# A fourth group of seven products in each FFN, with the quadrants in activation buffers

## The chip, the cores and the metric

The kernel runs on one core of one Trainium2 chip. The metric is the device time of one execution in microseconds (us). Each kernel is timed in several runs, and the median is compared. One further execution is taken by the hardware profiler, and all profile lines come from it.

Engines are called as in the profile: PE is the matrix engine, PEld its weight loads, DVE the vector engine, ACT the scalar engine, POOL GpSimd, SP the engine whose queue issues most transfers.

## The reference

A hybrid encoder of two layers works on 256 tokens of width 1024 in float32. Each layer has a gated linear attention branch, a grouped-query attention branch, a merge with an output projection, a SwiGLU FFN of hidden width 2816, and a gated per-layer embedding. The part that the change touches is the FFN:

```
gate, up = jnp.split(rms_norm(h, g_ffn_pre) @ w_ffn_in, 2, axis=-1)
h = h + rms_norm((jax.nn.silu(gate) * up) @ w_ffn_out, g_ffn_post)
```

`w_ffn_in` is 1024 x 5632, `w_ffn_out` is 2816 x 1024. The attention output projection `w_o_attn` (1024 x 1024) uses the same machinery as the FFN groups.

## The kernel before

**Numbers in two parts.** Every float32 operand of a product is kept as a high part (rounded by a cast) and a low part (what the rounding left). One product is three matmuls: high by high, high by low, low by high (`mm3`). The 256 tokens are two halves of 128 (`hf`).

**Weight units.** All weights are streamed once, as units of 1 MB (512 x 512 elements, in a tile of 128 x 2048). A unit is loaded by SP's queue into one of two `raw` tiles, then cut into two halves of 1024 columns. For each half ACT casts the high part into `wh` (L113) and DVE subtracts to get the low part `wl` (L109). There are four pairs of `wh` and `wl` (pool `wp`), and `Stream` counts how many are in use (`held`): a unit is made as soon as fewer than `depth` (4) are held, and given back when PE is done with it (`done`). A plain unit costs PE 24 matmuls of 512 columns, 12 for each token half.

**Groups of seven.** Where two by two quadrants of weights meet two by two quadrants of activations, eight products of quadrants can be replaced by seven products of sums (`seven`, and on the side of the weights `Stream.step`). A product of the seven is 12 matmuls. The activations' sums are made once per FFN (`sums`). On the side of the weights a group has four quadrants x, z, y, q of 1 MB. Step 1 splits x, then adds z to it (DVE) and adds y to z (a DMA that accumulates, from SBUF to SBUF). Step 2 splits x and adds y to it (DVE). Step 3 splits x and then adds q to it by two accumulating DMAs of 512 KB straight from HBM. Steps 4 to 7 split y, z, q (loaded as a raw unit) and x. Accumulating DMAs are issued by POOL. So x must be split in step 3, have q added, and be split again in step 7. On the side of the results DVE and ACT combine the products (`first_half`, copies and subtractions at L629 to L638), after product 6 for the first token half and after product 7 for the second.

Before the change x and z lie in a lent pair of `wh` and `wl`, so three pairs are left for splitting while a group is worked on; y lies in a tile of the pool `big` (nine tiles of 1 MB, which hold activations). The loads of a group wait for `ws.lend`, which the last step of the group before sets.

**The FFN.** The 2816 hidden columns are 11 blocks of 256. Blocks 0 and 1 are worked first, as plain units, first for one token half and then for the other. The strings `FFN` give the order after that: `u` is half a plain block of `w_ffn_in` (24 matmuls), a digit is a step of a group (two blocks, 12 matmuls), `o` is a unit of `w_ffn_out` (24 matmuls), `p` prepares the embedding. Each string has one group. Before: groups for blocks 2/3, 6/7 and 8/9 (`PAIRS`), plain blocks 4, 5 and 10 (`PLAIN`). The last three units of `w_ffn_out` come after the strings, again one token half after the other. `OUT` is the order of the units of `w_ffn_out`. The gated hidden activations are transposed by DMA on SP's queue (`turn_words`), those of the last group by PE, and lie in `big` tiles (`hid`).

**What sets the order.** The program is written in the order in which PE works; steps of transposes and the like are put in after so many "ticks". A planner then places each engine's instructions by priority and readiness in its own estimate of time, and gives out buffers. Each engine, and each DMA queue, runs its list in order, waiting on semaphores.

Of the kernel before, what the change touches and what calls it, by code (L numbers as in the profile page):

```python
# [34 lines left out]

FFN = "uu1u2u34u567" "uo12o34o5o67" "poo12o345o67"
MERGE = "GGGG1G2G34G5G67gggg"
PLAIN, PAIRS = (4, 5, 10), (2, 6, 8)  # L40
OUT = (0, 1, 2, 3, 4, 5, 10, 6, 7, 8, 9)

WAIT_LAST = (3, 4)
SENT, LANDED, NEXT = 3, 9, 2
# [7 lines left out]
def trunk_kernel(ctx: ExitStack, tc: tile.TileContext, a: dict, out: bass.AP):  # L52
# [58 lines left out]
    def split(hi, lo, src):  # L111

        cast = nc.scalar.copy(hi, src)  # L113
        vsub(lo, src, hi.bitcast(F32))
        return cast
# [56 lines left out]
            )  # L172
        ]

    plan = []
    for l in range(DEPTH):
        w = a["w_in"][l]
        plan += [unit_rows(w, n, C_RA, C_RA + 1056, 2 if l + n == 0 else 1) for n in range(4)]
        for c0 in (C_AK, C_GQ, C_GK, C_GV, C_GV + 512, C_GG, C_GG + 512):
            plan += [unit(w, kh, c0) for kh in range(2)]  # L180
        gates = [unit(w, kh, c0) for c0 in (C_GA, C_GA + 512, C_GB, C_GB + 512) for kh in range(2)]
        glas = [unit(a["w_o_gla"][l], kh, j * 512) for j in range(2) for kh in range(2)]
        pair = [unit(a["w_o_attn"][l], kh, j * 512) for kh in range(2) for j in range(2)]
        for x in MERGE:
            plan.append(gates.pop(0) if x == "G" else glas.pop(0) if x == "g" else (pair, int(x)))
        plan += [unit(a["w_out"][l], kh, j * 512) for kh in range(2) for j in range(2)]
        w = a["w_ffn_in"][l]
        blocks = [[unit_gate_up(w, kh, b) for kh in range(2)] for b in range(NBLK)]
        plan += blocks[0] + blocks[1]
        plains = [u for b in PLAIN for u in blocks[b]]  # L190
        pairs = [[unit(w, kh, c + b * 256) for kh in range(2) for c in (0, HIDDEN)] for b in PAIRS]
        outs = [unit_rows(a["w_ffn_out"][l], n) for n in OUT]
        for x in FFN.replace("p", ""):
            if x == "1":
                pair = pairs.pop(0)
            plan.append(plains.pop(0) if x == "u" else outs.pop(0) if x == "o" else (pair, int(x)))
        plan += outs
        plan += [unit_rows(a["w_ple_proj"][l], 0)]
        plan += [unit(a["w_ple_gate"][l], kh, j * 512) for kh in range(2) for j in range(2)]
# [14 lines left out]
    class Stream:  # L214
# [8 lines left out]
        def __init__(self, depth):  # L223
            self.depth, self.held, self.room, self.ready, self.open = depth, 0, 0, [], False
            self.loads, self.jobs, self.lend = [], [], False
            pairs = {}
            for item in plan:
                if callable(item):
                    x = Load(item)
                    self.loads.append(x)  # L230
                    self.jobs.append(lambda x=x: self.plain(x))
                else:
                    units, n = item
                    if n == 1:
                        b11, b12, b21, b22 = units
                        x, z = (Load(b, lambda tag=tag: self.lent(tag), tag == "wh") for b, tag in ((b11, "wh"), (b12, "wl")))
                        y, q = Load(b22, big), Load(b21)
                        pairs[id(units)] = x, y, z, q
                        self.loads += [x, y, z]
                    if n == 5:  # L240
                        self.loads.append(q)
                    self.jobs.append(lambda p=pairs[id(units)], n=n: self.step(n, *p))

        def lent(self, tag):

            if tag == "wh":
                self.held += 1
                self.lend = False
            return wp.tile([P, UNIT], F32R, tag=tag, name=nm("lent")).bitcast(F32)

        def load(self, between=lambda: None):
# [30 lines left out]
        def plain(self, x):  # L282
            return self.put(x)

        def made(self, x):
            for piece in self.put(x):
                self.cast = split(*piece)

        def step(self, n, x, y, z, q):
            def add(to, other):  # L290
                c = slice(0, 2048)
                nc.vector.tensor_tensor(out=to.raw[:, c], in0=to.raw[:, c], in1=other.raw[:, c], op=ALU.add)

            def sent(to, src):
                nc.gpsimd.dma_start(to.raw[:, :2048], src, accum_op=ALU.add)

            if n == 7:
                self.load()
            self.made((x, x, x, y, z, q, x)[n - 1])
            if n == 1:  # L300
                add(x, z)
                sent(z, y.raw[:, :2048])
            elif n == 2:
                add(x, y)
            elif n == 3:
                for dst, src in q.make(x.raw):
                    for c in (slice(0, 2), slice(2, 4)):
                        nc.gpsimd.dma_start(dst[:, c], src[:, c], accum_op=ALU.add)
            elif n == 7:
                self.held -= 1  # L310
                self.lend = True

# [1189 lines left out]
```

## Time and profile before

| | |
|---|---|
| median of the runs | 920.76 us (920.49 to 921.4) |
| the profiled execution's own time | 921.25 us |
| span in its profile | 919.1 us |
| PE busy | 904.6 us, 98% |
| DVE busy | 737.2 us, 80% |
| ACT busy | 643.9 us, 70% |
| DMA moved | 193.38 MB, 210 GB/s |

The time of the profiled execution is 2.15 us more than its span, which lies around the first and last instruction. Matmuls overlap in PE, so the mean duration of one (about 390 ns) is longer than the pace at which they follow each other. The pace is read from the chain of waits, which gives a stretch of matmuls with its length and count. DVE's and ACT's instructions overlap a little too: the distance between starts is some 0.07 us shorter than the duration.

### The profile page before, as it was taken

The page shows a single profiled execution, that of the slowest core. Times are in us where ns is not written, and L with a number is a line of the kernel's source. Part 1 is how long each engine was busy: PE and PEld are TensorE (multiplying, and loading weights), DVE is VectorE, ACT ScalarE, POOL GpSimd, SP SyncE. Part 2 cuts the span into 40 slices and gives each one's busy share as a digit, 9 for nine tenths or more (in the row PEclk, how much of TensorE's full clock was granted, in tenths as well). Part 3 has the DMA queues.
Part 4 walks back from the last instruction along what each step waited for, and adds up shares of the span by engine and source line. Part 5 has one row for each costly group of instructions (what it writes and reads, how often), then busy time and mean ns, then how long its engine had stood idle before and what let it go on. Part 6 is the DMA issues. An engine that isn't in the chain of part 4 may idle for free.

```text
span 919.1 us, 12313 instructions
## 1 busy us (share of the span) xinstructions
PE 904.6 (98%) x4561; PEld 768.3 (84%) x4561; DVE 737.2 (80%) x947; ACT 643.9 (70%) x1032; POOL 112.4 (12%) x174
## 2 busy tenths in 40 slices
PE   8999999999999999999999999999999999999996
PEld 6999888888888888888899988888888788878786
DVE  4798987977679796888689789688786798968874
ACT  4658777964568796776665686878656787957663
POOL 2410201140010100010023002111001010101000
PEclk9999999999999999999999999999999999999999
DMA  6555356986489998966555524399675999979541
GB/s 218 182 193 180 117 163 231 229 241 234 144 243 256 279 273 250 301 194 240 184 176 184 190 91 148 128 290 234 208 247 173 274 230 290 261 284 243 200 167 46
DMA packets 123290, 193.38 MB, mean 210 GB/s; under 512 B 33431, under 2 KB 56471, under 8 KB 122206
## 3 DMA queue, kind: packets, MB, share of 16 engines
q1 hardware_dynamic: 117726, 175.81, 59.3%
q0 software_dynamic: 5504, 16.78, 10.1%
q8 instruction: 36, 0.59, 0.3%
q14 instruction: 24, 0.20, 0.1%
HBM read 175.80 MB, written 1.05 MB: 192 GB/s over the span
## 4 chain that ended last, share of the span: by engine, by line
PE 80%; ACT 6%; DMA 5%; DVE 4%; issue 2%; POOL 2%; SPq 0%; POOLq 0%; ACTq 0%; DVEq 0%
PE acc_0ffnin L97 10%; PE acc_1ffnin L97 10%; PE acc_0ffnin L581 5%; PE acc_1gate L97 5%; PE acc_0gate L97 5%; PE acc_1ffnin L581 4%; PE acc_1gqk L97 3%; PE acc_0rq L97 2%; PE acc_0gqk L97 2%; PE acc_1ple L97 2%; PE acc_1gg L97 2%; PE acc_0gg L97 2%; PE acc_0v L97 2%; PE acc_1v L97 2%; PE acc_1merge L97 2%; PE acc_0merge L97 2%
## 5 line engine op out<-in xcount | busy, mean ns | idle before, releaser
L97 PE MATMUL acc_1ffnin<-wh_1ffnin,big_1ffnin 128*128 128x512 f32 x176 | 56.5, 392 | 0.1
L97 PE MATMUL acc_0ffnin<-wh_0ffnin,big_0ffnin 128*128 128x512 f32 x176 | 56.2, 391 | 0.0
L109 DVE TENSOR_TENSOR wl_1ffnin<-raw_1ffnin,wh_1ffnin 128x1024 fp32r<-128x1024 f32 x38 | 44.9, 1220 | 12.3 <-ACT wh_1ffnin L113 12.3
L109 DVE TENSOR_TENSOR wl_0ffnin<-raw_0ffnin,wh_0ffnin 128x1024 fp32r<-128x1024 f32 x38 | 44.9, 1221 | 10.5 <-ACT wh_0ffnin L113 10.2
L113 ACT CAST wh_1ffnin<-raw_1ffnin 128x1024 fp32r<-128x1024 f32 x38 | 38.3, 1050 | 17.7 <-DMA raw_1ffnin<-in_w_ffn_out_dram 9.1
L113 ACT CAST wh_0ffnin<-raw_0ffnin 128x1024 fp32r<-128x1024 f32 x38 | 38.4, 1050 | 16.8 <-DMA raw_0ffnin<-in_w_ffn_out_dram 7.8
L109 DVE TENSOR_TENSOR wl_1ffnin<-lent_1ffnin,wh_1ffnin 128x1024 fp32r<-128x1024 f32 x30 | 35.5, 1220 | 4.9 <-ACT wh_1ffnin L113 4.7
L109 DVE TENSOR_TENSOR wl_0ffnin<-lent_0ffnin,wh_0ffnin 128x1024 fp32r<-128x1024 f32 x30 | 35.5, 1221 | 4.8 <-ACT wh_0ffnin L113 4.7
L97 PEld LDWEIGHTS acc_1ffnin<-wh_1ffnin,big_1ffnin 128*128 128x128 f32 x176 | 33.0, 188 | 7.2 <-ACT wh_1ffnin L113 0.5
L97 PEld LDWEIGHTS acc_0ffnin<-wh_0ffnin,big_0ffnin 128*128 128x128 f32 x176 | 33.0, 188 | 6.9 <-DVE big_0ffnin L109 0.2
L113 ACT CAST wh_1ffnin<-lent_1ffnin 128x1024 fp32r<-128x1024 f32 x30 | 30.3, 1049 | 8.6 <-issue 2.9
L113 ACT CAST wh_0ffnin<-lent_0ffnin 128x1024 fp32r<-128x1024 f32 x30 | 30.3, 1050 | 8.4 <-issue 2.9
L97 PE MATMUL acc_1ffnin<-wl_1ffnin,big_1ffnin 128*128 128x512 f32 x88 | 34.4, 391 | 0.8 <-DVE wl_1ffnin L109 0.8
L97 PE MATMUL acc_0ffnin<-wl_0ffnin,big_0ffnin 128*128 128x512 f32 x88 | 34.5, 392 | 0.3 <-DVE wl_0ffnin L109 0.3
L581 PE MATMUL acc_0ffnin<-wh_0ffnin,mid_0ffnin 128*128 128x512 f32 x96 | 31.0, 390 | 0.0
L581 PE MATMUL acc_1ffnin<-wh_1ffnin,mid_1ffnin 128*128 128x512 f32 x96 | 31.0, 390 | 0.0
L97 PE MATMUL acc_0ffnin<-wh_0ffnin,big_0wout 128*128 128x512 f32 x96 | 30.4, 389 | 0.0
L97 PE MATMUL acc_1ffnin<-wh_1ffnin,big_1wout 128*128 128x512 f32 x96 | 30.3, 389 | 0.0
L97 PE MATMUL acc_0rq<-wh_start,big_start 128*128 128x384 f32 (+1 forms) x96 | 25.4, 350 | 1.5 <-ACT big_start L124 1.5
L97 PE MATMUL acc_1rq<-wh_0ple,big_0ple 128*128 128x384 f32 (+1 forms) x96 | 23.5, 325 | 0.0
L581 PE MATMUL acc_1ffnin<-wh_1ffnin,big_1wout 128*128 128x512 f32 x72 | 23.1, 389 | 0.0
L581 PE MATMUL acc_0ffnin<-wh_0ffnin,big_0wout 128*128 128x512 f32 x72 | 23.1, 389 | 0.0
(745 smaller groups left out, 3011.7 us busy)
## 6 DMA issues: line engine op xcount, KB each, us to landing
raw_0ffnin<-in_w_ffn_out_dram SPq DMA_DIRECT2D x11, 1024.0 KB, 5.1
raw_1ffnin<-in_w_ffn_out_dram SPq DMA_DIRECT2D x11, 1024.0 KB, 5.1
lent_0ffnin<-in_w_ffn_in_dram SPq DMA_DIRECT2D x6, 1024.0 KB, 7.5
lent_1ffnin<-in_w_ffn_in_dram SPq DMA_DIRECT2D x6, 1024.0 KB, 6.0
raw_0rq<-in_w_in_dram SPq DMA_DIRECT2D x4, 1024.0 KB, 5.1
raw_0v<-in_w_in_dram SPq DMA_DIRECT2D x4, 1024.0 KB, 5.1
raw_0merge<-in_w_out_dram SPq DMA_DIRECT2D x4, 1024.0 KB, 5.2
raw_0wout<-in_w_ffn_in_dram SPq DMA_DIRECT2D x8, 512.0 KB, 4.6
```

The source lines that it names most:

```text
L97: return nc.tensor.matmul(o, lhsT, rhs, start=start, stop=stop)
L109: nc.vector.tensor_tensor(out=out, in0=in0, in1=in1, op=ALU.subtract)
L113: cast = nc.scalar.copy(hi, src)
L581: nc.tensor.matmul(o, x, y, start=first and k + n == 0, stop=k == 3 and n == 2, skip_group_check=not first)
```

## The change

- The strings `FFN` become four, each with one group: blocks 2/3, 4/5, 6/7 and 8/9. Only block 10 (and blocks 0 and 1) stay plain. Both half-blocks `u` and one `o` lie in the first string, two `o` in the second and third, three in the fourth. The units of `w_ffn_out` outside the strings are the same three. `OUT` is reordered so that block 10 comes third.
- x and z of the FFN groups (`roomy`) lie in `big` tiles, not in `wh`/`wl`; so all four pairs are there for splitting. `lend` is set after step 6. The group of `w_o_attn` keeps its lent pair.
- The sums of steps 1 and 2 are made by halves of 1024 columns, each right behind the split of that half.
- The third sum is made by DMA for every group in the list `added`; since that list holds them all, the other path (`n == 5 and not far`, a DVE sum) is not used.

```diff
-FFN = "uu1u2u34u567" "uo12o34o5o67" "poo12o345o67"
+FFN = "u1u2o34567" "1o2o34567" "p1o2o34567" "1o2o34o567"
-PLAIN, PAIRS = (4, 5, 10), (2, 6, 8)
-OUT = (0, 1, 2, 3, 4, 5, 10, 6, 7, 8, 9)
+PLAIN, PAIRS = (10,), (2, 4, 6, 8)
+ADDED = (2, 4, 6, 8)
+OUT = (0, 1, 10, 2, 3, 4, 5, 6, 7, 8, 9)
...
-        def lent(self, tag):
-
-            if tag == "wh":
-                self.held += 1
-                self.lend = False
+        def lent(self, tag, i):
+
+            self.lend = False
+            if i in roomy:
+                return big()
+            self.held += tag == "wh"
             return wp.tile([P, UNIT], F32R, tag=tag, name=nm("lent")).bitcast(F32)
...
-        def made(self, x):
-            for piece in self.put(x):
+        def made(self, x, other=None):
+            for j, piece in enumerate(self.put(x)):
                 self.cast = split(*piece)
+                if other:
+                    self.add(x, other, slice(j * 1024, (j + 1) * 1024))
...
-            self.made((x, x, x, y, z, q, x)[n - 1])
+            self.made((x, x, x, y, z, q, x)[n - 1], {1: z, 2: y}.get(n))
             if n == 1:
-                add(x, z)
                 sent(z, y.raw[:, :2048])
-            elif n == 2:
-                add(x, y)
-            elif n == 3:
+            elif n == 3 and far:
                 for dst, src in q.make(x.raw):
                     for c in (slice(0, 2), slice(2, 4)):
                         nc.gpsimd.dma_start(dst[:, c], src[:, c], accum_op=ALU.add)
-            elif n == 7:
+            elif n == 5 and not far:
+                self.add(x, q)
+            elif n == 6 and roomy_:
+                self.lend = True
+            elif n == 7 and not roomy_:
                 self.held -= 1
                 self.lend = True
```

More of the change, by code (lines that the diff above doesn't have):

```diff
@@ L173, in unit_rows @@
         ]
-    plan = []
+    plan, added, roomy = [], [], []
     for l in range(DEPTH):
@@ L183, in trunk_kernel @@
         pair = [unit(a["w_o_attn"][l], kh, j * 512) for kh in range(2) for j in range(2)]
+        added.append(id(pair))
         for x in MERGE:
@@ L195, in trunk_kernel @@
                 pair = pairs.pop(0)
+                roomy.append(id(pair))
+                if PAIRS[-1 - len(pairs)] in ADDED:
+                    added.append(id(pair))
             plan.append(plains.pop(0) if x == "u" else outs.pop(0) if x == "o" else (pair, int(x)))
@@ L235, in __init__ @@
                         b11, b12, b21, b22 = units
-                        x, z = (Load(b, lambda tag=tag: self.lent(tag), tag == "wh") for b, tag in ((b11, "wh"), (b12, "wl")))
+                        x, z = (Load(b, lambda tag=tag, i=id(units): self.lent(tag, i), tag == "wh") for b, tag in ((b11, "wh"), (b12, "wl")))
                         y, q = Load(b22, big), Load(b21)
@@ L241, in __init__ @@
                         self.loads.append(q)
-                    self.jobs.append(lambda p=pairs[id(units)], n=n: self.step(n, *p))
-        def lent(self, tag):
-            if tag == "wh":
-                self.held += 1
-                self.lend = False
+                    self.jobs.append(lambda p=pairs[id(units)], n=n, f=id(units) in added, r=id(units) in roomy: self.step(n, f, r, *p))
+        def lent(self, tag, i):
[3 more added lines that the diff above has]
+            self.held += tag == "wh"
             return wp.tile([P, UNIT], F32R, tag=tag, name=nm("lent")).bitcast(F32)
@@ L283, in plain, with add, step @@
             return self.put(x)
-        def made(self, x):
-            for piece in self.put(x):
+        def made(self, x, other=None):
+            for j, piece in enumerate(self.put(x)):
                 self.cast = split(*piece)
[L289 to L292, printed above, removed]
+                if other:
+                    self.add(x, other, slice(j * 1024, (j + 1) * 1024))
+        def add(self, to, other, c=slice(0, 2048)):
+            nc.vector.tensor_tensor(out=to.raw[:, c], in0=to.raw[:, c], in1=other.raw[:, c], op=ALU.add)
+        def step(self, n, far, roomy_, x, y, z, q):
             def sent(to, src):
```

## The prediction, made before the change was run

> **What bounds the kernel now.** I read the page first, then PE's waits, the chain of waits, the busy time by stretches of the FFN, and the order of time on DVE and POOL.
>
> ```profile
> span 919.1 us, 12313 instructions
> PE 904.6 (98%) x4561; PEld 768.3 (84%) x4561; DVE 737.2 (80%) x947; ACT 643.9 (70%) x1032; POOL 112.4 (12%) x174
> ...
> PE acc_1ffnin L97 <- DVE wl_1ffnin L109: 0.8, 1, 0.8
> ...
> PE acc_0ffnin L97 <- DVE wl_0ffnin L109: 0.3, 1, 0.3
> ```
>
> PE is the bound, and in the FFN it waits for the weights' low parts hardly at all. The chain gives PE's pace:
>
> ```profile
> 266.28 24.94 PE acc_0ffnin L97 x107
> 291.22 2.72 PE acc_0ffnin L581 x12
> ```
>
> Twelve matmuls, one product of a group, take 2.72 us; a plain unit of 24 takes 5.44. The first group begins at 291.22 behind two plain units, so the first string begins at 280.3. The strings of layer 0 by stretches (length; busy PE, PEld, DVE, ACT, POOL; clock; DMA share; GB/s), and the last two of layer 1:
>
> ```profile
> 280.18:326.42 46.24, 46.24 (x205) 38.30 (x204) 40.43 (x44) 37.34 (x52) 3.42 (x3) 1.00 0.97 253
> 326.42:373.38 46.96, 46.69 (x206) 38.38 (x205) 38.14 (x38) 34.64 (x42) 3.29 (x3) 1.00 0.92 282
> 373.38:414.68 41.30, 41.30 (x186) 34.19 (x185) 36.84 (x34) 30.74 (x35) 4.31 (x4) 1.00 0.85 232
> ...
> 775.30:823.10 47.80, 46.98 (x206) 38.37 (x205) 38.65 (x38) 35.52 (x43) 3.36 (x3) 1.00 0.94 278
> 823.10:866.50 43.40, 42.70 (x192) 35.04 (x191) 37.48 (x36) 31.40 (x37) 3.33 (x3) 1.00 0.86 243
> ```
>
> PE is full, but DVE is busy 81 to 89% and the DMA engines 85 to 97%. Whatever shortens PE's work here and lengthens theirs meets them soon.
>
> **What the change removes.** Blocks 4 and 5 were four plain units, 21.76 us of PE; as a group they are seven products, 19.04. That saves 2.72 us in each layer, 5.44 in all. It is worth this only if PE stays fed.
>
> **What it adds on DVE and ACT.** Three more splits per layer, two weight sums, the group's result sums. The rows:
>
> ```profile
> 276.35 2.37 DVE L109 TENSOR_TENSOR wl_0ffnin<-raw_0wout,wh_0ffnin 128x1024 fp32r<-128x1024 f32 x2 [0.51 <-ACT wh_0ffnin L113]
> ...
> 298.08 2.35 DVE L109 TENSOR_TENSOR wl_0ffnin<-raw_0ffnin,wh_0ffnin 128x1024 fp32r<-128x1024 f32 x2
> 300.36 0.42 DVE L109 TENSOR_TENSOR big_0ffnin<-mid_0ffnin,big_0ffnin 128x256 fp32r<-128x256 f32 x1
> 300.69 2.35 DVE L109 TENSOR_TENSOR wl_0ffnin<-lent_0ffnin,wh_0ffnin 128x1024 fp32r<-128x1024 f32 x2
> ...
> 331.19 0.69 DVE L106 TENSOR_TENSOR t_0ffnin<-mid_0ffnin,t_0ffnin 128x512 f32<-128x512 f32 x1
> 331.79 2.29 DVE L292 TENSOR_TENSOR lent_0ffnin<-lent_0ffnin,lent_0ffnin 128x2048 f32<-128x2048 f32 x1
> 333.99 0.75 DVE L106 TENSOR_TENSOR t_0ffnin<-acc_0ffnin,t_0ffnin 128x256 f32<-128x256 f32 x2
> ...
> 342.71 2.36 DVE L109 TENSOR_TENSOR wl_0ffnin<-lent_0ffnin,wh_0ffnin 128x1024 fp32r<-128x1024 f32 x2
> ```
>
> By starts, a unit's two subtractions take 2.28 us, 1.14 a half; a 512-column operation 0.60, a 256-column one 0.33, a whole weight sum 2.20. A sum by halves isn't in the trace; a subtraction of 1024 columns has the same shape, so 1.14, and two halves cost 0.08 more than the whole: nothing. What halves may gain is that the next cast needn't await the whole sum; I count that as nothing too, at most one cast (1.05, below) in each of steps 1 and 2 where DVE waits.
>
> New second string, "1o2o34567": PE 7 x 2.72 + 2 x 5.44 = 29.92 us. DVE: nine units 20.52, four half sums 4.56, three result sums, two gate products and two splits of turned activations, seven times 0.60 = 4.2; together 29.3. The old second string confirms it: 38.14 busy, less three units (6.84) and a plain block's products and split (about 1.3), is 30.0 by durations. So DVE has no slack in the two inner strings. ACT: 34.64 less three units of two casts (6.3) is 28.3 or less, some slack. In the first string PE has 35.36, in the last 35.36 with a DVE need of 31.6.
>
> **Buffers and loads.** Nine `big` tiles: u2 two, up to three `hid` tiles alive, x, y, z of this group, and x of the next before this one ends. Tiles of consumed hidden blocks come free as each `o` ends, in time for the next z and y; I cost this at nothing, covered by the 13.6 us or more of products 3 to 7 between that `o` and the next group. The loads wait in SP's queue only for these tiles; the raw loads and transposes stand behind them there, so a late tile costs those a wait as well.
>
> **The loop that decides.** x is split in step 3, has q added by DMA, and is split again in step 7, now with only steps 4, 5, 6 in between. Before, a plain unit or two lay there as well.
>
> ```profile
> 344.30 2.41 POOL L308 DMA_DIRECT2D lent_0ffnin<-in_w_ffn_in_dram  x2 [8.71 <-DVE wl_0ffnin L109]
> ...
> lent_0ffnin<-in_w_ffn_in_dram POOLq DMA_DIRECT2D x2, 512.0 KB, 10.3
> ...
> lent_0ffnin<-in_w_ffn_in_dram POOLq DMA_DIRECT2D x2, 512.0 KB, 11.1
> ...
> lent_0ffnin<-in_w_ffn_in_dram POOLq DMA_DIRECT2D x2, 512.0 KB, 7.5
> ...
> lent_1ffnin<-in_w_ffn_in_dram POOLq DMA_DIRECT2D x2, 512.0 KB, 10.0
> ...
> lent_1ffnin<-in_w_ffn_in_dram POOLq DMA_DIRECT2D x2, 512.0 KB, 12.3
> ...
> lent_1ffnin<-in_w_ffn_in_dram POOLq DMA_DIRECT2D x2, 512.0 KB, 8.2
> ...
> DMA to landing us min/median/max: 6.1/9.1/13.6
> ...
> L113 ACT CAST wh_0ffnin<-raw_0ffnin 128x1024 fp32r<-128x1024 f32 x38 | 38.4, 1050 | 16.8 <-DMA raw_0ffnin<-in_w_ffn_out_dram 7.8
> ```
>
> The lines with KB are the landing times of the six groups in order, three for each layer; the line below them is over all sixteen such DMAs, the attention projection's too. The first half's DMA is issued at 344.30, 0.45 after the first subtraction begun at 342.71 gives way (342.71 + 1.14 = 343.85); the second 1.2 later, that is 0.5 after the unit's split. With landing time A, step 7's second half is cast (1.05) and subtracted (1.14) by 0.5 + A + 2.2 after step 3. DVE's list then runs on in order: one result sum 0.6, step 1 4.56 and two 512s 1.2, `o` 2.28, step 2 4.56 and one 0.6, `o` 2.28, two turned splits 1.2, step 3 2.28: 19.56. The loop takes A + 22.3 us, and PE's string 29.92. Up to A = 7.6 it costs nothing; above, each turn falls back by A - 7.6.
>
> There are three turns per layer (from each string's step 3 to the next one's). DVE enters with a lead: from 276.35 it has to do u, 1, u, 2, o, 3 (18.2), five operations of 512 for the activations' sums (3.0), four turned splits and three products of 256 (2.3), so is done at 299.9; PE comes to step 3 at 280.3 + 21.8 = 302.1, and needs only the first half, 1.14 earlier. Lead 3.3.
>
> The DMA wait isn't seen in this position, so its bounds: 7.5 (the emptiest neighbour) gives no stall; 12.3 (behind two or three fresh loads) gives 3 x 4.7 - 3.3 = 10.8 us per layer. I take 9.1, the median of all sixteen, one below the FFN groups' own: before, each step 3 had a raw load and a y just issued ahead of it; now the next group's loads go out earlier, as their tiles come free. Stall 3 x 1.5 - 3.3 = 1.2 per layer, 2.4 in all.
>
> [...]
>
> **Sum.** 921.25 (the profiled execution: 919.1 and 2.15 around it) - 5.44 + 2.4 = 918.2; the median of the runs stands 0.49 below that execution, so **917.7 us**, 3.1 (0.33%) faster.
>
> **Rivals.** *Fully hidden.* If A stays under 8.7, three turns eat no more than the lead: 920.76 - 5.44 = 915.3. For it: 7.5 in the third group. Against: DVE's waits of ACT, which I left out.
>
> *The accumulating DMA takes the place of the plain units (slower).* Place: cast of step 7 waiting for x, with DVE and ACT behind it in order. It outweighs the gain when three turns cost 2.72 + 3.3 = 6.0 per layer, that is 2.0 each, A above 9.6. At A = 10.3: 4.8 per layer, 920.76 - 5.44 + 9.6 = 924.9; at 11.1: 7.2 and 929.7. For it: four of the six groups landed at 10.0 or later. Against: the lead may be larger with four split pairs instead of three.
>
> *The DMA engines themselves become the bound.*
>
> ```profile
> q0 software_dynamic: 688, 2.10, 24.4%
> ```
>
> One group's accumulations took 24.4% of the second string, 11.5 us of all sixteen engines. Shares of the three old strings: 0.97 x 46.24 + 0.92 x 46.96 + 0.85 x 41.30 = 123.2 us. With 11.5 more it is 134.7, against PE's new 130.6. If none of it moves ahead of the strings, 4.1 per layer is lost: 920.76 - 5.44 + 8.2 = 923.5; if x and z of the first group go ahead of it (two loads of 1.05 MB, 6.8 us at the second string's 282 GB/s over its share 0.92), nothing is lost. Half of it, 919.4, is no change that can be told.
>
> *The change does not do what it says*: nine tiles don't suffice and x arrives late. Then the old pattern returns, one wait of a raw load (7.8 us of ACT's idle in 38 casts, little of it reaching PE): about 921.
>
> **Chances.** Forecast 0.40; hidden 0.17; slower by the loop 0.27; DMA bound or tiles late 0.16. Within 0.2% (1.84 us, about what a measurement of this kernel can tell from no change) fall part of the forecast's own spread (a landing 0.4 longer adds 2.4 us) and most of the last case. Faster 0.46, same 0.22, slower 0.32. The likeliest case alone holds 916 to 921; the range for 8 in 10 reaches from just under the hidden case to the crowded landing: 914.8 to 927.
>
> **What would show it.** PE: 24 fewer matmuls in all, 4537. DVE in the inner strings over 95% busy. A wait of ACT's cast in step 7 for an accumulating DMA, and behind it PE waits on `wl` in steps 1 and `o` of the next string: small if right, 4 us or more per layer if the slower rival is. Landing of the accumulating DMAs near 9. If DVE's idle time is before other casts than step 7's, the loop is the wrong cause. If PE waits for raw or `big` loads, it is the DMA engines or the tiles.

## The result, and the profile after

The changed kernel takes 953.79 us (median of 4 runs, 949.25 to 957.09); the kernel before, beside it, 920.85 us (920.49 to 921.4). The ratio is 1.0361, with a 95% interval of 1.0338 to 1.0383: it is 3.6% slower, where 917.7 us was forecast.

The head of the page of the changed kernel:

```profile
span 951.9 us, 12344 instructions
PE 911.1 (96%) x4537; PEld 769.0 (81%) x4537; DVE 761.1 (80%) x985; ACT 656.2 (69%) x1042; POOL 116.7 (12%) x180
```

PE has its 24 matmuls less (4537 instead of 4561) and is busy 6.5 us longer. At the pace of before 4537 matmuls would be 904.6 x 4537 / 4561 = 899.8 us, so the matmuls have become slower, by 11.3 us in all (not evenly: in the turns below, those at a clock of 1.00 have 0.228 to 0.229 us of busy time for each, close to the 0.226 and 0.227 of the first two strings of layer 0 before; those at 0.91 to 0.95 have 0.234 to 0.244). PE's idle time rose from 919.1 - 904.6 = 14.5 us to 40.8. Against the span that the change was to give (919.1 - 5.44 = 913.7) 38.2 us are missing.

They are missing in the strings of the FFN. The third sum of a group is issued once per string, so the distance from one such issue to the next is one turn of the loop that the prediction described. The changed kernel by these turns, three in layer 0 and three in layer 1 (columns as in the prediction's table of strings):

```profile
296.14:330.12 33.98, 31.65 (x138) 25.56 (x137) 30.34 (x33) 27.51 (x35) 3.34 (x3) 1.00 0.83 213
330.12:366.07 35.95, 32.40 (x135) 26.00 (x134) 29.60 (x30) 25.61 (x30) 3.31 (x4) 0.95 1.03 267
366.07:400.53 34.46, 31.86 (x140) 25.39 (x139) 30.05 (x31) 26.03 (x31) 3.32 (x3) 1.00 0.93 254
756.20:791.76 35.56, 31.54 (x138) 25.36 (x138) 30.43 (x33) 28.45 (x38) 3.33 (x3) 1.00 0.85 215
791.76:829.36 37.60, 32.43 (x133) 26.27 (x131) 29.55 (x30) 25.63 (x30) 3.35 (x4) 0.91 1.03 253
829.36:865.01 35.65, 33.03 (x141) 27.01 (x140) 30.05 (x31) 25.93 (x31) 3.31 (x4) 0.95 0.92 249
```

The six turns last 213.2 us; PE needs 6 x 29.92 = 179.5. That is 33.7 us, nearly all of the loss. PE, DVE and ACT all have idle time in every turn: none of them is the bound. The DMA engines' share is 0.83 to 1.03 (the reckoning can come out over 1); what that is worth is taken up below.

The chain of waits of the changed kernel (start, length, what was under way), its entries of a DMA in the FFN:

```profile
297.26 11.56 DMA big_0ffnin<-in_w_ffn_in_dram
331.32 14.01 DMA big_0ffnin<-in_w_ffn_in_dram
367.19 12.60 DMA big_0ffnin<-in_w_ffn_in_dram
400.19 7.31 DMA mid_0ffnin<-t_0ffnin
...
752.12 11.35 DMA mid_1ffnin<-t_1ffnin
792.90 15.72 DMA big_1ffnin<-in_w_ffn_in_dram
830.48 13.78 DMA big_1ffnin<-in_w_ffn_in_dram
864.66 14.94 DMA mid_1ffnin<-t_1ffnin
```

The five `big` entries are the second of the two accumulating DMAs of a group, issued 1.1 to 1.2 us behind the first; the three `mid` entries are DMA transposes of turned activations. The longest waits of ACT and of PE (us in all, times, longest), in the profile's views of waits:

```profile
ACT mid_1ffnin L435 <- DMA mid_1ffnin<-t_1ffnin: 25.9, 5, 10.1
ACT mid_0ffnin L435 <- DMA mid_0ffnin<-t_0ffnin: 11.3, 5, 3.9
...
ACT wh_0ffnin L114 <- DMA big_0ffnin<-in_w_ffn_in_dram: 5.6, 4, 2.2
```

```profile
PE acc_1ffnin L589 <- ACT mid_1ffnin L642: 9.8, 3, 5.2
PE acc_1ffnin L98 <- ACT big_1ffnin L114: 7.3, 1, 7.3
PE acc_0ffnin L589 <- ACT mid_0ffnin L642: 4.0, 2, 3.2
PE acc_0ffnin L589 <- DVE mid_0ffnin L110: 3.6, 4, 2.0
```

So ACT stands at two places: at the cast of step 7 (L114) for the third sum, which was foreseen, and far longer at the copy behind a DMA transpose (L435; L427 before), which was not. Behind it in ACT's list stand the copy that frees a product's accumulator (L642) and the next casts, and PE waits for those.

### The profile page after: what moved, and what is told of

It reads as the page before. It is cut to its first block, busy times and chain, and to the rows that moved or that the text cites. A ratio compares the mean times of both kernels' runs of the same rounds, so it can differ in the third digit from the quotient of the medians.

```text
span 951.9 us, 12344 instructions
## 1 busy us (share of the span) xinstructions
PE 911.1 (96%) x4537; PEld 769.0 (81%) x4537; DVE 761.1 (80%) x985; ACT 656.2 (69%) x1042; POOL 116.7 (12%) x180
## 4 chain that ended last, share of the span: by engine, by line
PE 61%; DVE 13%; DMA 13%; ACT 6%; issue 4%; POOL 2%; SPq 0%; POOLq 0%; DVEq 0%; ACTq 0%
PE acc_1ffnin L98 5%; PE acc_1gate L98 5%; PE acc_0gate L98 5%; DMA big_0ffnin<-in_w_ffn_in_dram 4%; PE acc_0ffnin L98 4%; DVE wl_0ffnin L110 3%; DMA big_1ffnin<-in_w_ffn_in_dram 3%; DVE wl_1ffnin L110 3%; DMA mid_1ffnin<-t_1ffnin 3%; PE acc_1gqk L98 2%; PE acc_0rq L98 2%; PE acc_0gqk L98 2%; PE acc_1ple L98 2%; PE acc_1gg L98 2%; PE acc_0gg L98 2%
## 5 line engine op out<-in xcount | busy, mean ns | idle before, releaser
L114 ACT CAST wh_0ffnin<-big_0ffnin 128x1024 fp32r<-128x1024 f32 x48 | 49.3, 1052 | 16.7 <-DVE big_0ffnin L298 10.5
L110 DVE TENSOR_TENSOR wl_0ffnin<-big_0ffnin,wh_0ffnin 128x1024 fp32r<-128x1024 f32 x48 | 56.4, 1220 | 4.5 <-ACT wh_0ffnin L114 4.5
L114 ACT CAST wh_1ffnin<-big_1ffnin 128x1024 fp32r<-128x1024 f32 x48 | 49.3, 1052 | 13.5 <-DVE big_1ffnin L298 10.1
L110 DVE TENSOR_TENSOR wl_1ffnin<-big_1ffnin,wh_1ffnin 128x1024 fp32r<-128x1024 f32 x48 | 56.3, 1220 | 2.3 <-ACT wh_1ffnin L114 2.3
L589 PE MATMUL acc_1ffnin<-wh_1ffnin,mid_1ffnin 128*128 128x512 f32 x128 | 44.6, 416 | 9.8 <-ACT mid_1ffnin L642 9.8
L589 PE MATMUL acc_0ffnin<-wh_0ffnin,mid_0ffnin 128*128 128x512 f32 x128 | 42.6, 400 | 4.0 <-ACT mid_0ffnin L642 4.0
L110 DVE TENSOR_TENSOR wl_1ffnin<-raw_1ffnin,wh_1ffnin 128x1024 fp32r<-128x1024 f32 x34 | 40.3, 1221 | 2.2 <-ACT wh_1ffnin L114 2.2
L110 DVE TENSOR_TENSOR wl_0ffnin<-raw_0ffnin,wh_0ffnin 128x1024 fp32r<-128x1024 f32 x34 | 40.3, 1219 | 1.5 <-ACT wh_0ffnin L114 1.4
L589 PEld LDWEIGHTS acc_1ffnin<-wh_1ffnin,mid_1ffnin 128*128 128x128 f32 x128 | 26.0, 203 | 16.5 <-ACT mid_1ffnin L642 10.9
L114 ACT CAST wh_1ffnin<-raw_1ffnin 128x1024 fp32r<-128x1024 f32 x34 | 34.2, 1046 | 6.8 <-DMA raw_1ffnin<-in_w_ffn_in_dram 1.8
L114 ACT CAST wh_0ffnin<-raw_0ffnin 128x1024 fp32r<-128x1024 f32 x34 | 34.2, 1047 | 5.0 <-DVE mid_0ffnin L110 3.3
L589 PE MATMUL acc_0ffnin<-wh_0ffnin,big_0wout 128*128 128x512 f32 x96 | 31.6, 397 | 3.6 <-DVE mid_0ffnin L110 3.6
L589 PEld LDWEIGHTS acc_0ffnin<-wh_0ffnin,mid_0ffnin 128*128 128x128 f32 x128 | 24.6, 192 | 9.8 <-ACT mid_0ffnin L642 4.6
L589 PE MATMUL acc_1ffnin<-wh_1ffnin,big_1wout 128*128 128x512 f32 x96 | 30.5, 391 | 2.0 <-DVE mid_1ffnin L110 2.0
L435 ACT COPY mid_1ffnin<-mid_1ffnin 128x1024 uint16<-128x1024 uint16 (+1 forms) x10 | 11.2, 1122 | 25.9 <-DMA mid_1ffnin<-t_1ffnin 25.9
L110 DVE TENSOR_TENSOR big_1ffnin<-mid_1ffnin,big_1ffnin 128x512 fp32r<-128x512 f32 (+1 forms) x11 | 6.3, 591 | 28.0 <-ACT big_1ffnin L114 27.9
```

Of the source, the lines that this page charges most:

```text
L110: nc.vector.tensor_tensor(out=out, in0=in0, in1=in1, op=ALU.subtract)
L435: nc.scalar.copy(z16.rearrange("p (c s) -> p s c", s=2), r16.rearrange("p (s c) -> p s c", s=2))
L589: nc.tensor.matmul(o, x, y, start=first and k + n == 0, stop=k == 3 and n == 2, skip_group_check=not first)
```

## The experiments

Theories at the start: the loop through the third sum's accumulating DMA (L); the late DMA transposes, at which ACT's list stands (T); and DVE, which the change fills (V). All experiments start from the changed kernel unless said otherwise. Batches were run on one chip each, with the kernel before beside them (919.61, 920.44, 920.2, 920.21 and 919.95 us).

### Taking the two transfers away

Third sum left out (`e1`), transposes left out (`e2`), both (`e3`), and the second `o` of each string moved behind product 4, so that more lies between steps 3 and 7 (`e4`):

```diff
# e1
-            elif n == 3 and far:
+            elif n == 3 and far and not roomy_:
# e2
-            nc.sync.dma_start_transpose(out=r16..., in_=w16)
+            if far: r16 = w16
+            else: nc.sync.dma_start_transpose(out=r16..., in_=w16)
# e4
-FFN = "u1u2o34567" "1o2o34567" "p1o2o34567" "1o2o34o567"
+FFN = "u1u234o567" "1o234o567" "p1o234o567" "1o2o34o567"
```

> The changed kernel without the third sum of the FFN groups: the two accumulating DMAs of step 3 are left out, so step 7 splits x without q and the FFN's output is wrong. All else, the transposes by DMA too, stays. Theory L (the loop: ACT and DVE wait in order at step 7 for the accumulating DMA, which lands 11 to 16 us after its issue): most of the 33 us go, 920 to 928. Theory T (the DMA transposes land late, and ACT's copy behind them holds up ACT's list): only what the accumulations took from the transposes comes back, 935 to 945. Theory V (DVE is simply full in the inner strings): nothing changes, 948 to 955.

> The changed kernel without the FFN's DMA transposes: ACT's second copy reads the untransposed words, so the output is wrong, but every copy, split and accumulating DMA stays. Theory T: ACT's 37 us of waiting for transposes go, 918 to 928. Theory L: the accumulating DMA stays late behind the loads of the next group, 938 to 950. Theory V: 948 to 955.

> Both left out together, the third sum and the transposes (output wrong). Theories L and T together: the 5.4 us of matmuls saved should show, 914 to 919. Theory V: DVE's work is unchanged, so PE still starves, above 930.

> The changed kernel, complete, with one plain unit moved from before step 3 to between steps 4 and 5 in the first three strings (u1u234o567, 1o234o567, p1o234o567, the last as it was). Theory L: each loop has 5.4 us more of PE's time and one split more between step 3 and step 7, so three turns of each layer gain up to 2.3 us or more, 930 to 942. Theory T: the transposes and the loads of the next group are no further apart, 948 to 955. Theory V: steps 1 and 2, the heaviest for DVE, come closer together, 952 to 960.

Measured: `e1` 922.12 us (ratio 1.0022, interval 1.0008 to 1.0036), `e2` 940.92 (1.0238, 1.0221 to 1.0256), `e3` 913.18 (0.9931, 0.9916 to 0.9946), `e4` 949.66 (1.0335, 1.0299 to 1.0371).

`e3` shows that the change's arithmetic on the three engines is right: with neither transfer PE is fed, and DVE holds out at 98%. The inner strings of layer 0 in `e3`, by stretches:

```profile
310.00:390.00 80.00, 79.85 (x354) 65.42 (x353) 78.75 (x79) 67.11 (x78) 3.57 (x4) 1.00 0.75 233
```

`e1` came out as theory L said; `e2` too, so T alone is out, and V is out by all three; `e3` lies a little below the 914 to 919 expected. So the loss of 40.6 us between `e3` and the changed kernel comes from the two transfers. The third sum alone, with no transposes (`e2` less `e3`), costs 27.7; the transposes alone (`e1` less `e3`) 8.9; both together some 4 more than the sum (1.2 of it lies between the two batches' runs of the kernel before).

What the third sum costs alone is the predicted loop. The chain of waits of `e2`, its accumulating DMAs:

```profile
295.86 12.55 DMA big_0ffnin<-in_w_ffn_in_dram
330.90 12.57 DMA big_0ffnin<-in_w_ffn_in_dram
365.34 12.61 DMA big_0ffnin<-in_w_ffn_in_dram
755.08 12.59 DMA big_1ffnin<-in_w_ffn_in_dram
790.52 12.88 DMA big_1ffnin<-in_w_ffn_in_dram
825.27 12.81 DMA big_1ffnin<-in_w_ffn_in_dram
```

Its issues on POOL, the ends of the row of turns in layer 0:

```profile
294.74 2.47 POOL L312 DMA_DIRECT2D big_0ffnin<-in_w_ffn_in_dram  x2 [13.41 <-DVE wl_0ffnin L110]
...
399.95 2.45 POOL L312 DMA_DIRECT2D big_0ffnin<-in_w_ffn_in_dram  x2 [10.55 <-ACT wh_0ffnin L114]
```

Three turns take 105.21 us, 35.07 each. The prediction's formula, landing time plus 22.3, gives 12.58 + 22.3 = 34.9. The length of the loop is as it was drawn, but the landing time that goes into it is 12.6, where 9.1 was taken. Its parts are not all as drawn: in the first turn of a layer the chain leaves DVE's list behind the landing and goes through PE's matmuls and ACT's casts (317.13 to 328.91 in `e2`), so there the agreement is partly luck. By the prediction's own rule (three turns less the lead of 3.3) that is 3 x (34.88 - 29.92) - 3.3 = 11.6 us per layer, 23.2 in all, of the 27.7 measured; the rest is not accounted for.

The same run shows what goes with the late landing. The issues of the third group and of the last, of layer 0 (KB each, median of the two transfers in us):

```profile
big_0ffnin<-in_w_ffn_in_dram POOLq DMA_DIRECT2D x2, 512.0 KB, 11.2
...
big_0ffnin<-in_w_ffn_in_dram POOLq DMA_DIRECT2D x2, 512.0 KB, 6.8
```

The second transfer of the third group took 12.6 us, that of the last 7.7 (8.6 in layer 1). Behind the last no next group is loaded. So the loads of the next group go with 4 to 5 us of the landing; no run took them away by themselves.

`e4` should have shortened the loop by the formula: in the first two turns of a layer one `o`, 2.28 us of DVE's list, then lies before the landing, and the third turn has 5.44 us more of PE's work. Theory L's 930 to 942 is missed (949.66 against 953.79, the ranges overlap); T's 948 to 955 holds it. The third sum is gone from the chain of waits of `e4`. In its place stand, among others, loads of the next group (10.44, 10.32 and 13.71 us), transposes (7.05, 8.57 and 13.27) and a load for the embedding (12.28). So to take the third sum off the path, with all transfers left where they are, gives next to nothing: others beside it are late too.

### Is it DVE, the moment, the bytes or the accumulating?

Third sum on DVE (`e5`), the next group's loads let go behind step 7 (`e9`), half of the third sum's bytes (`e10`), plain copies in POOL's queue instead of accumulating ones (`e11`):

```diff
# e5
-ADDED = (2, 4, 6, 8)
+ADDED = ()
# e9: lend set behind step 7 instead of step 6
-            elif n == 6 and roomy_:
-                self.lend = True
-            elif n == 7 and not roomy_:
-                self.held -= 1
+            elif n == 7:
+                self.held -= not roomy_
                 self.lend = True
# e10
-                    for c in (slice(0, 2), slice(2, 4)):
+                    for c in ((slice(0, 1), slice(2, 3)) if roomy_ else (slice(0, 2), slice(2, 4))):
# e11
-                        nc.gpsimd.dma_start(dst[:, c], src[:, c], accum_op=ALU.add)
+                        nc.gpsimd.dma_start(dst[:, c], src[:, c])   # FFN groups
```

> The changed kernel, complete, with the third sum of the FFN groups made by DVE (one addition of 2048 columns, about 2.2 us, behind step 5) instead of two accumulating DMAs. Theory L (step 7 waits for the accumulating DMA): the wait goes and DVE gets 2.2 us more in a string of 29.9 that already needs 29.3, so a stall of some 1.6 us per inner string remains, 922 to 932. Theory V (DVE is full and that is what costs): 952 to 965. The DMA transposes stay and keep their 7 to 13 us.

> The changed kernel, complete, with the loads of the next group's x, z, y let go one step later (behind step 7, as in the kernel before, not behind step 6). Theory B (the accumulating DMA is late only because three loads of 1 MB are issued in the same microseconds): it lands near 9 us instead of 11 to 16 and the time falls to 930 to 943. Theory L without B: landing and time stay, 948 to 956; loads that come too late would add to it.

> The changed kernel with only half of q added in step 3 of the FFN groups (two accumulating DMAs of 256 KB in place of 512 KB; the output is wrong). Theory L: the wait is the landing time of these DMAs, and with half the bytes it is some 3 to 5 us shorter in each of three turns per layer: 925 to 938. If the cost is the fixed part of such a DMA, or DVE, 945 to 953.

> The changed kernel with plain copies in place of the accumulating DMAs of step 3, from the same queue, of the same bytes and with the same dependences (x is overwritten by q, so the output is wrong). If it is the read-modify-write of the accumulation that makes them slow beside other traffic, they land in 5 to 8 us and the time is 922 to 935; if it is GpSimd's queue or the traffic itself, landing stays near 11 to 13 and the time 945 to 955.

Measured: `e5` 921.5 us (1.0022, 1.0003 to 1.0041), `e9` 952.04 (1.0344, 1.0296 to 1.0392), `e10` 946.13 (1.0281, 1.0259 to 1.0303), `e11` 951.13 (1.0344, 1.0311 to 1.0378).

`e5` gives DVE 2.2 us per group more to do and is 32 us faster than the changed kernel: a full DVE isn't the main cause. It also takes nearly all of the loss against the kernel before away, as leaving the third sum out does (922.12). In `e5` itself DVE is full: from 326 to 389 us it is busy 63.00 us of 63, so there it is the bound.

`e9` decides nothing, for its edit did not move the loads. The three loads of the next group in SP's queue, first in the changed kernel, then in `e9` (start of the first, length of the three issues):

```profile
331.16 3.46 SPq L269 DMA_DIRECT2D big_0ffnin<-in_w_ffn_in_dram  x3
...
328.74 4.01 SPq L269 DMA_DIRECT2D big_0ffnin<-in_w_ffn_in_dram  x3
```

The third sum was issued at 330.12 and at 327.70, so both times the loads begin 1.04 us behind it (the second string of layer 0). Whether their moment matters stays open.

`e10` and `e11` shorten the landing of the third sum in most groups, but `e10` misses theory L's 925 to 938, and `e11` the 922 to 935 that were expected if accumulating were the cost. The second of its two transfers lands, in the four groups of layer 0, after 7.1, 10.8, 9.6 and 8.1 us in `e10` (in `e11` after 8.1, 11.8, 13.9 and 9.5), so the loop costs less, yet the time hardly moves: there the transposes take over. The three turns of layer 0 in `e10` are 36.8, 33.9 and 35.0 us, where landing plus 22.3 gives 29.4, 33.1 and 31.9. The chain of waits of `e10` holds a transpose in each turn, and no transfer of the third sum; the entries of layer 0:

```profile
291.77 12.56 DMA mid_0ffnin<-t_0ffnin
332.27 7.70 DMA mid_0ffnin<-t_0ffnin
366.13 8.39 DMA mid_0ffnin<-t_0ffnin
401.16 9.41 DMA mid_0ffnin<-t_0ffnin
```

ACT waits 39 us (`e10`) and 43 us (`e11`) at the copies behind the transposes, against 37 in the changed kernel and 8 in `e5`.

### Which queue

The same plain copies at the same place in SP's queue (`e12`) and in ACT's (`e13`), and the third sum and the transposes both in ACT's queue (`e15`):

```diff
# e12
-                        nc.gpsimd.dma_start(dst[:, c], src[:, c], accum_op=ALU.add)
+                        nc.sync.dma_start(dst[:, c], src[:, c])     # FFN groups
# e13: the same with nc.scalar
# e15: e13, and
-            nc.sync.dma_start_transpose(out=r16..., in_=w16)
+            (nc.scalar if far else nc.sync).dma_start_transpose(out=r16..., in_=w16)
```

> The changed kernel, but the third sum's two 512 KB transfers of the FFN groups go as plain copies through SP's queue (the addition is left out: q overwrites x, so the FFN's numbers are wrong; every wait and every byte is the same). Beside the plain copies through POOL's queue (951.1 us), only the queue differs. Theory Q (a transfer in POOL's queue is what slows the DMA transposes beside it and itself lands in 9 to 10 us): the copies land in 6 us or less, the transposes in 6 or less, ACT's waits for the turned words fall from 43 us to under 12, time 915 to 928. Rival T (any 1 MB at this place, whatever queue): 940 to 955, with transposes again at 7 or more. Caveat stated beforehand: SP's queue now stands still until step 3 is split, so the loads behind it start up to 2 us later.

> As the run with SP's queue, but the two plain copies of the third sum are issued by ACT (the addition is left out here too). The SP queue with its loads and transposes is as in the changed kernel. Theory Q: 915 to 930, transposes land in 6 us or less. Rival T: 940 to 955. If SP's run is slow and this one fast, it was the standstill of SP's queue in that run; if both are slow at transposes of 7 us or more, POOL's queue is acquitted.

> As the run with the third sum's plain copies on ACT's queue (947.4 us; the addition of q is left out), and the DMA transposes of the FFN are issued by ACT too, so that third sum and transposes share one queue, while the loads of 1 MB stay alone in SP's. Theory F (transposes suffer when the third sum runs beside them from another queue; in one queue they go one after the other): as fast as all in SP's queue, 918 to 928, transposes land in 7 us or less. Rival G (the third sum and the transposes must share the queue of the loads, because only there do the 3 MB of loads issued behind them wait their turn): 940 to 955, with the transposes late again.

Measured: `e12` 922.47 us (1.0024, 1.0008 to 1.004), `e13` 947.41 (1.0293, 1.0265 to 1.0321), `e15` 981.29 (1.0649, 1.0628 to 1.0669).

The three kernels `e11`, `e12` and `e13` move the same bytes between the same buffers, and lie 29 us (POOL's queue against SP's) and 25 us (ACT's against SP's) apart. Theory Q, as it was put, falls by `e13`, and its rival T by `e12`. So a third sum need not be in POOL's queue to cost; but `e13` isn't a clean twin of `e12`, since the issues then stand in ACT's own list (at 327.10 the two reach over 1.45 us), and what that costs was not taken apart. The profile's view of DMAs has the third sum's copies in `e12` (KB each, median us to landing):

```profile
big_0ffnin<-in_w_ffn_in_dram SPq DMA_DIRECT2D x8, 512.0 KB, 6.6
```

Layer 1 has 6.6 too. Of the second copies, those of the second to fourth group of layer 0 have a landing in the trace: 5.9, 7.0 and 6.2. That is below the 7.6 at which, by the prediction's formula, the loop begins to cost. The turns of layer 0 in `e12` are 31.33, 31.23 and 32.84 us, still 1.3 to 2.9 above PE's 29.92; on the chain there stand transposes of 6.51 to 7.63 us.

The transposes show the other half. The last one of layer 1's strings (blocks 6/7, second token half) is issued within 3 us of the last group's third sum, except where that is left out or DVE's work. Its landing time:

| kernel | third sum | transpose lands after |
|---|---|---|
| changed | accumulating, POOL's queue | 14.9 us |
| `e10` | half the bytes, POOL's queue | 12.0 |
| `e11` | plain, POOL's queue | 11.3 |
| `e13` | plain, ACT's queue | 9.4 |
| `e12` | plain, SP's queue | 7.5 |
| `e1` | left out | 6.3 |
| `e23` (below) | on DVE | 4.7 |

At this place no group follows, so no x, z or y of a next group is in flight; a raw load of 1 MB and another of 512 KB are issued in the stretch. The changed kernel there, in order of time (start, length, engine):

```profile
864.66 2.49 SPq L422 DMA_TRANSPOSE mid_1ffnin<-t_1ffnin  x1
865.01 2.46 POOL L312 DMA_DIRECT2D big_1ffnin<-in_w_ffn_in_dram  x2 [9.89 <-ACT t_1ffnin L416]
...
879.62 1.33 ACT L435 COPY mid_1ffnin<-mid_1ffnin 128x1024 uint16<-128x1024 uint16 x1 [10.10 <-DMA mid_1ffnin<-t_1ffnin]
880.82 1.12 ACT L114 CAST big_1ffnin<-mid_1ffnin 128x512 fp32r<-128x512 f32 x2
881.46 1.29 DVE L110 TENSOR_TENSOR big_1ffnin<-mid_1ffnin,big_1ffnin 128x512 fp32r<-128x512 f32 x2 [11.43 <-ACT big_1ffnin L114]
```

ACT stands 10.1 us, DVE 11.4. In `e13` too the chain holds only transposes in the strings, 7.58 to 13.43 us long, and none of the third sum. The transfers of this stretch, 864 to 880 us, in 40 slices (busy tenths of the DMA engines, and what they moved):

```profile
DMA  9497799899899957229999999999989749798999
GB/s 317 105 251 42 162 312 198 338 343 348 307 333 339 286 98 88 72 56 178 59 50 49 55 57 59 70 63 83 63 52 82 58 58 144 94 133 183 236 246 287
DMA packets 3061, 2.54 MB, mean 159 GB/s; under 512 B 2172, under 2 KB 2172, under 8 KB 3046
```

From the 20th to the 31st slice the engines are busy to 8 tenths or more and move 49 to 83 GB/s.

`e15` doesn't decide between its theories, and lies far outside the ranges of both. It brought a cost of its own: issuing a transpose, 1.2 to 1.4 us mostly, held ACT for 7.16 us at 379.43, 4.78 at 817.04 and 7.23 at 863.33, and casts stand behind it (18.5 and 14.9 us of ACT's idle time before casts, listed as issue). So whether the third sum must share a queue with the transposes or with the loads stays open.

### What ACT's standing costs

ACT's copies of the turned words 6 steps later, everywhere (`e8`; with the third sum on DVE, `e14`), then in the FFN alone (`e18`):

```diff
# e8, e14
-SENT, LANDED, NEXT = 3, 9, 2
+SENT, LANDED, NEXT = 3, 15, 2
# e18
-            yield LANDED
+            yield LANDED + (6 if far and 'ffnin' in part[0] else 0)
```

> The changed kernel complete, with one number changed: the copies of the turned words (ACT) are put in after 15 steps of PE instead of 9. Theory L (the late transposes cost time because ACT works its list in order and stands at this copy, with a free accumulator and the next casts behind it): the waits at that copy fall from 37 us to under 12, the transposes still land in 7 us or more, and about the same amount of time is given back: 925 to 938 (step 7's wait for the third sum stays). Rival R (transposes only show the congestion, the third sum and the loads are as late and stop ACT or DVE at their own places): the waits move to casts that wait for DMAs or DVE, time 945 to 955.

> The third sum of the FFN groups on DVE (921.5 us by itself), and the copies of the turned words put in 6 steps later; complete. Theory L: the 8 us that ACT still waited at that copy go, and half or more of it reaches the end: 914 to 918. Rival: these waits were covered, 920 to 923.

> The changed kernel complete, with ACT's copies of the turned words put in 6 steps later in the FFN alone (the earlier run moved them in the merge stage too, where it cost 10.6 us per layer; its FFN stages were 377.2 us together against 387.9 in the changed kernel). Theory L (ACT standing at these copies costs a part, some 11 of the 38 us): 940 to 946. Rival: 950 to 955.

Measured: `e8` 964.17 us (1.0477, 1.0442 to 1.0511), `e14` 938.93 (1.0213, 1.0197 to 1.0229), `e18` 948.81 (1.0286, 1.0253 to 1.0319).

`e8` and `e14` were ill made: the number also holds for the merge stage, and the output projection there grew from 23.8 us to 34.4 and 33.9 in `e8`, 34.4 and 33.4 in `e14`. `e18` leaves that out. The waits at the copies disappear, and the median is 5 us lower than 953.79 (the ranges overlap: 943.64 to 958.48 against 949.25 to 957.09). The waits of ACT in `e18`:

```profile
ACT wh_0ffnin L114 <- DMA big_0ffnin<-in_w_ffn_in_dram: 16.4, 7, 4.1
ACT wh_1ffnin L114 <- DMA big_1ffnin<-in_w_ffn_in_dram: 13.5, 6, 4.4
```

ACT now stands at step 7's cast for the third sum instead. Theory L's range of 940 to 946 is missed, and the wait was mostly moved: two late transfers, one in-order list, and the later of them sets the pace.

### A version without the crossing transfers

Third sum on POOL as an engine (`e16`), the same with the later copies (`e20`), and a DMA for the first group of each layer alone, where no group's transposes lie beside it (`e21` with, `e23` without the later copies; plain blocks' transposes do lie beside it):

```diff
# e16, e20: ADDED = (), and
-                self.add(x, q)
+                nc.gpsimd.tensor_tensor(out=x.raw[:, :2048], in0=x.raw[:, :2048], in1=q.raw[:, :2048], op=ALU.add)
# e21, e23
-ADDED = (2, 4, 6, 8)
+ADDED = (2,)
# e20, e21: also the edit of e18
```

> Complete kernel: the third sum of the FFN groups is neither a DMA nor DVE's work, but one addition of 128x2048 on POOL in step 5 (q comes as a raw load). It takes the 1 MB of crossing transfers away, as with DVE (921.5 us; FFN of layer 0 177.0 us against 173.7 with neither third sum nor transposes), but without DVE's 2.2 us per group. If DVE's load is what remains of the loss: 914 to 918, faster than before. Rival (POOL and DVE slow each other, or POOL's addition takes so long that step 7 waits for it): 920 to 930.

> Third sum on POOL and the later copies together; complete. If both small rests go: 912 to 916, faster than before and than either alone. Rival: equal to the third sum on POOL alone, within 1.5 us.

> Complete: of the third sums of the FFN only the first group's of each layer stays a DMA (there no group's transposes lie beside it), the other three are made by DVE, and ACT's copies of the turned words come 6 steps later in the FFN. If DVE's 2.2 us per group is what is left of the loss (FFN stages 355 us together with all on DVE, 353.9 with the later copies, 347.5 with neither third sum nor transposes), the first group gives up to 2.2 us per layer of lead: 914.5 to 918. Rival: one crossing DMA per layer costs as much as it relieves: 919 to 924.

> The same without the later copies (they stay at 9 steps): 916 to 920 if the copies matter by 1 us, as they did with all sums on DVE; rival as there: 920 to 926.

Measured: `e16` 936.66 us (1.0178, 1.0162 to 1.0194), `e20` 956.83 (1.0388, 1.0373 to 1.0404), `e21` 925.11 (1.0063, 1.0045 to 1.0081), `e23` 918.58 (1.0002, 0.9976 to 1.0027).

`e16` and `e20` miss both their ranges. POOL's addition takes 4.6 to 8.9 us in `e16`, 7.3 in the mean, and DVE is held up beside it. The second string of `e16`, in order of time:

```profile
329.43 8.90 POOL L314 TENSOR_TENSOR big_0ffnin<-big_0ffnin,raw_0ffnin 128x2048 f32<-128x2048 f32 x1 [13.05 <-ACT wh_0ffnin L114]
...
335.34 4.14 DVE L110 TENSOR_TENSOR big_0ffnin<-mid_0ffnin,big_0ffnin 128x512 fp32r<-128x512 f32 x2 [1.51 <-ACT big_0ffnin L114]
```

Two such subtractions took 1.29 us in the changed kernel. `e23` is the best of the complete variants of the four groups and no different from the kernel before: the 5.44 us that PE saves don't come out. Its twelve times spread from 916.3 to 926.5 us, and the profiled execution (925.8) is near the upper end; in it the second DMA of layer 1's only third sum landed 17.0 us after its issue. By the prediction's count of DVE (29.3 of 29.92 us in the inner strings) 2.2 us more in each of three groups would be enough to use PE's saving up, and `e5`, where DVE is never idle from 326 to 389 us, bears that out. The later copies, which I expected to help by 1 us, cost 6.5 (`e21` against `e23`) and 20 (`e20` against `e16`); why stays open. No complete version of the four groups beat the kernel before.

## Why the prediction was wrong

**PE's saving** was right in count (4537 matmuls). `e3`, 913.18 us, is 6.4 below the kernel before beside it, where 5.44 were to come out.

**DVE's and ACT's need** were right: 98% of DVE in `e3`, as 29.3 of 29.92 says. ACT's 67.11 of 80 us there are 25.1 per string, under the 28.3 that was its bound. In the changed kernel DVE was not over 95% busy in the inner strings, since it waited (79 to 89% in the six turns).

**The loop that decides** was the right loop, at the right place, and its length (landing plus 22.3) comes out. The step that failed is the term "I take 9.1, the median of all sixteen". That term was too small for two reasons. First, the second half of x lands last, and step 7 can't end before it. The trace of before shows this. Its group of 344.30, the first of its two DMAs by itself, then both:

```profile
lent_0ffnin<-in_w_ffn_in_dram POOLq DMA_DIRECT2D x1, 512.0 KB, 10.0
...
lent_0ffnin<-in_w_ffn_in_dram POOLq DMA_DIRECT2D x2, 512.0 KB, 11.1
```

The mean of the two is 11.1, the first 10.0, so the second took 12.2. The prediction read the line with x2 as one landing time, and took the median over firsts and seconds. Read in this way, the seconds of the six groups took 11.0, 12.2, 9.0, 10.7, 13.6 and 8.9, in the mean 10.9. By the prediction's rule that is 3 x 3.3 - 3.3 = 6.6 per layer, 928.5 us: outside the range, but far from 953.79. So the misreading is 1.8 of what was missing.

Second, it argued that the landing would get shorter, "now the next group's loads go out earlier"; it got longer: 11.56 to 15.72, mean 13.5, in the five chain rows. The loads did go out earlier, and that put them beside the third sum. Before, x and z of the next group were issued at 367.97 and 368.39, 24 us behind the third sum of 344.30, with a raw load and a y just ahead of it; in the changed kernel three loads of 1 MB begin 1.04 us behind the one of 330.12, with two transposes ahead of it. `e2` has 12.6 with such loads and no transposes, and 7.7 and 8.6 where no next group is loaded. By the prediction's rule 13.5 gives 3 x 5.9 - 3.3 = 14.4 us per layer, and 921.25 - 5.44 + 28.8 - 0.49 = 944.1; 9.7 us are left for what the sum did not have. Turn by turn it is closer still: the five landings plus 22.3 are 33.9, 36.3, 34.9, 38.0 and 36.1; the turns that hold them were 33.98, 35.95, 34.46, 37.60 and 35.65. In the sixth turn the chain goes through a transpose (752.12); the second transfer took 13.1 there, which gives 35.4, and the turn was 35.56.

**The slower rival** named this mechanism and priced it up to A = 11.1, 929.7 us; its own upper bound of 12.3 would have given 10.8 per layer, 936.9, and the far end of the line that it showed (13.6) 14.7, 944.7. The range stopped at 927.0 because the centre was set too low.

**What the sum did not have.** First, the transposes in SP's queue: "a late tile costs those a wait as well" was all it said of them, and their copies in ACT's list were not costed. At the end of layer 1's strings one of them held ACT for 10.1 us, DVE for 11.4 and PE for 7.3, and where the third sum was shortened (`e10`, `e11`, `e13`) they kept the time up. Second, PE's clock. Around that stall the stretches of the changed kernel are (the clock stands before the last two columns):

```profile
860.00:870.00 10.00, 10.00 (x46) 8.29 (x45) 10.00 (x10) 9.33 (x11) 2.46 (x2) 1.00 1.19 254
870.00:880.00 10.00, 4.15 (x19) 3.10 (x17) 0.03 (x1) 0.38 (x1) 0.00 (x0) 0.84 1.26 103
880.00:890.00 10.00, 8.52 (x26) 6.77 (x27) 8.37 (x9) 8.30 (x11) 0.00 (x0) 0.65 0.66 192
890.00:900.00 10.00, 10.00 (x48) 8.31 (x47) 8.19 (x10) 6.48 (x8) 0.00 (x0) 1.00 0.78 263
```

PE's last matmul before the stall ended at 874.15 and the next began at 881.48. The same view in steps of half a us has the clock at 1.00 up to 876.5, at 0.72 in the step from there, at 0.50 from 877.0 to 886.5 and at 1.00 again from 887.0. So in this stall it fell 2.4 to 2.9 us after PE's last matmul and came back 5.0 to 5.5 us after the first one behind the stall. In the stretch from 880 to 890 it was 0.65 in the mean, and 8.52 us of work held 26 matmuls instead of some 39. In the whole run the clock was 0.986 against 0.998. Worked out from these two means, 951.9 x 0.014 - 919.1 x 0.002 = 11.5 us of clock were lost (an estimate), some of it while PE stood, so it is of the size of the 11.3 us of slower matmuls above. Here 26.3 us more of idle time of PE came with 11.3 us of slower matmuls; from what length of a stall on the clock falls, no run shows.

**The DMA engines as the bound** and **the change not doing what it says** were not it as they were put. `e11` and `e12` move the same bytes by plain copies, with DMA shares of 0.78 to 0.92 and 0.77 to 0.97 in the turns of layer 0, and are 29 us apart, so the bytes alone don't set the time. In layer 0 ACT's four waits for a `big` tile from HBM (5.6 us in all) are those of step 7. The test named for "the loop is the wrong cause" (DVE idle before other casts than step 7's) would have misled: DVE's longest idle times were behind the transposes' copies (L110 of `big`, 27.9 and 13.8 us in the two layers), while the turns kept the length of the loop.

**What stays open.** Why the queue decides, and how much of the late landing the loads of the next group make by themselves. Shown is that third sum and transposes are late together when they are in different queues, and less late when both are in SP's, which holds the loads too. The third sum's landing (median in layer 0, then in layer 1) and that of the transpose of the table were 11.3, 13.4 and 14.9 us in the changed kernel, 9.6, 9.5 and 11.3 in `e11`, 8.1, 7.5 and 9.4 in `e13`, and 6.6, 6.6 and 7.5 in `e12`. So in a queue of their own the copies of `e13` landed no earlier than in the shared one of `e12`, and in the kernel's time the choice of queue was worth 25 to 29 us.

## What to carry to other kernels

When a step needs two transfers, read the landing of the one that lands last, not the median over both; a row with x2 hides it. Before work that separates a transfer's issue from its use is taken out, write the loop through it as landing time plus list, and price it at the far end of what the trace shows. Ask which loads the change will put beside it: here the same transfer took 12.6 us beside a group's loads and 7.7 without them. A transfer that is moved beside others may make them late too, so see who waits for those, in which in-order list, and what stands behind.

## What the runs showed that was not expected

- Two accumulating DMAs of 512 KB landed 12.55 to 12.88 us behind the issue of the second in `e2`, in each of the six turns on the chain: hardly any spread, with the next group's loads and no transposes about. In the last group of each layer, without such loads, it was 7.7 and 8.6. Plain copies in SP's queue took 6.6 (median of `e12`).
- With one transpose, one third sum and two loads under way, the DMA engines were busy at 49 to 83 GB/s for over 4 us; 2172 of the 3061 packets of that stretch were under 512 bytes.
- The same copies in SP's queue and in POOL's differ by 29 us in the kernel's time, in SP's and in ACT's by 25.
- A DMA transpose issued by ACT held ACT for 1.2 to 7.2 us.
- An addition of 128x2048 took POOL 4.6 to 8.9 us and DVE 2.28; beside it two subtractions of 128x512 on DVE took 4.14 us instead of 1.29.
